# The recurrence's state-reading matmuls widened from 64x32 to 64x64 tiles

## The chip, the cores and the metric

The kernel runs on one core of one Trainium2 chip, in one launch. The metric is device time in microseconds (us), the median of three runs. The profile is of one execution, whose time is given beside its span.

## What is computed

Two blocks of two layers each are run one after the other on 512 tokens of width 1024. The first block has feed-forwards, an mLSTM layer and a dilated attention layer. The second block's layers mix a bidirectional RWKV-7 recurrence (6 heads of 64), a grouped-query attention and a neighbourhood attention; a context of 256 tokens goes through the same recurrence first and hands its end states on. What the change touches is the recurrence, which the reference writes as a scan over tokens in both directions:

```python
S_f, y_f = lax.scan(_rwkv7_step, S0_f, (r, decay[:, :, 0], kd[:, :, 0], v, kk, bd[:, :, 0]))
S_b, y_b = lax.scan(_rwkv7_step, S0_b, (r, decay[:, :, 1], kd[:, :, 1], v, kk, bd[:, :, 1]),
                    reverse=True)
return S_f, S_b, y_f + y_b
```

Each step multiplies a 64x64 state per head by its decay, takes out what the state holds along one direction and adds new key-value products.

## The kernel before

The kernel does the recurrence in chunks of 32 tokens. `rwkv_a`, `rwkv_b` and `rwkv_c` prepare, for a direction r, all that doesn't depend on the state: among it `zk`, three tiles (one for two heads, one head in the upper and one in the lower 64 partitions) of 128 x n with 32 columns for each chunk, copied out of PSUM at L1907; `be`, the tokens' write vectors; and `UV`, the values, in rows of 64 of which 32 are the state's correction.

`rwkv_d` (from L1910) then runs the chain, step by step, for the forward direction r = 0 and the backward direction r = 1 side by side. In a step a direction takes chunk g (ascending for r = 0, descending for r = 1) and does this:

- a first group of six matmuls (three tiles, two halves, L1932): 64 partitions of `zk`, the chunk's 32 columns, as the stationary operand, and the state S as the moving one, 64 columns. The product lands in 32 rows of the PSUM tile `pw`, at row 0 or 64;
- on GpSimd, `keep`, the state times the chunk's decay (L1934);
- on VectorE, the subtraction of `pw` from `UV` in two halves (L1941);
- a second group of six matmuls on 64x64 tiles (L1946), `be` against the corrected `UV`, into `pn`;
- on VectorE, the sum of `pn` and `keep`, which is the new S (L1950).

After every fourth step, where outputs are wanted, the y matmuls follow: 24 a direction with the states kept from the four steps (64x32 tiles, L1967) and 12 with `UV` on 128x64 tiles (L1973). All of these are float32 matmuls, which TensorE runs in two passes, each with a weight load and a matmul of its own in the profile.

`rwkv_d` is run four times: for the context of either layer (8 steps; the first layer's with outputs) beside the first block's feed-forward, and for the latents of either layer (16 steps) beside the attention.

The order of instructions is not that of the program's text. All operations are recorded, and a planner (`simulate`, L485, called by `schedule`, L588) puts them in order for the five engines: a list scheduler with costs for each operation (`_cost`, L408), which goes backward and forward three times. For TensorE it adds 0.14 us where the tile shape changes (`RETILE`, L274), and among ready matmuls it prefers one of the current shape if its priority is within 3.0 us (`STAY`, L278) of the most urgent. It also hands out the working tiles, kind "t" (64 slots), "S" (16), "ps" (8) and others (`SLOTS`, L265), and may put a plain copy of 60 columns or more on ScalarE or on VectorE (L381). Since every instruction is issued from one place, all lines of the profile are L632.

Of the kernel before, what the change touches and what calls it, by code (L numbers as in the profile page):

```python
# [16 lines left out]
P = 128  # L17
# [618 lines left out]
class Prog:  # L636
# [47 lines left out]
    def row(self):  # L684
        return self.t2((4, T))
# [1193 lines left out]
    def rwkv_c(self, d, q, r):  # L1879

        n, nb = d["n"], d["nb"]
        UV = d["UV"][r]
        q["zk"] = []
        for j in range(3):
            pb = [self.ps((P, nb, 64)) for _ in range(2)]
            for b in range(nb):
                for par in range(2):
                    for a in range(2):
                        self.mm(pb[par][64 * a:64 * a + 64, b], q["EB"][2 * j + par][:, 2 * b + a], UV[:, b, a, 2 * j + par])
            bv = self.t2((P, 2, nb, 64))  # L1890
            for par in range(2):
                self.act(bv[:, par], pb[par])
            pu, pz = self.ps((P, nb, 2, 64)), self.ps((P, n))
            for par in range(2):
                h, o = 2 * j + par, 64 * par
                x = self.t2((P, nb, 4, 32))
                self.mul(x, q["Z"][:, :, nb * h:nb * h + nb].rearrange("p t b -> p b t").unsqueeze(2).to_broadcast([P, nb, 4, 32]),
                         self.k("bd4").unsqueeze(1).unsqueeze(3).to_broadcast([P, nb, 4, 32]))
                x = x.rearrange("p b c t -> p b (c t)")
                for b in range(nb):  # L1900
                    self.mm(pu[:, b, par], x[:, b], bv[:, par, b])
                    self.mm(pz[o:o + 64, P * b:P * b + P], q["kt"][j][:, b, o:o + 64], x[:, b])
                for c in range(4):
                    ro = 64 * (c % 2 ^ par)
                    self.act(UV[ro:ro + 32, :, c // 2, h], pu[32 * c:32 * c + 32, :, par], scale=-1.0)
            zk = self.t2((P, n))
            self.act(zk, pz)  # L1907
            q["zk"].append(zk)

    def rwkv_d(self, d, qs, S):  # L1910

        n, nb, need_y = d["n"], d["nb"], d["need_y"]
        if need_y:
            d["y"] = [None] * nb
        both = [(j, par) for j in range(3) for par in range(2)]
        row = lambda c, par: 64 * (c % 2 ^ par)
        S = list(S)
        old, pw, pn = [{}, {}], [None] * 2, [None] * 2  # L1920
        for step in range(4 * nb):
            gs = (step, 4 * nb - 1 - step)
            keep = []
            for r, g in enumerate(gs):
                c = g % 4
                if step % 4 == 0:
                    ps = self.ps((P, 2, 3, 64))
                    pw[r], pn[r] = ps[:, 0], ps[:, 1]
                old[r][c] = S[r]
                for j, par in both:  # L1930
                    o, ro = 64 * par, row(c, par)
                    self.mm(pw[r][ro:ro + 32, j], qs[r]["zk"][j][o:o + 64, 32 * g:32 * g + 32], S[r][o:o + 64, j])  # L1932
                keep.append(self.new("S", (P, 3, 64)))
                self.nc.gpsimd.tensor_tensor(out=keep[r], in0=S[r], in1=qs[r]["D"][:, g].unsqueeze(2).to_broadcast([P, 3, 64]),  # L1934
                                             op=ALU.mult)
            for r, g in enumerate(gs):
                b, c = g // 4, g % 4
                for par in range(2):
                    ro = row(c, par)
                    u = d["UV"][r][ro:ro + 32, b, c // 2, par::2]  # L1940
                    self.tt(u, u, pw[r][ro:ro + 32], ALU.subtract)  # L1941
            for r, g in enumerate(gs):
                b, c = g // 4, g % 4
                for j, par in both:
                    o, ro = 64 * par, row(c, par)
                    self.mm(pn[r][o:o + 64, j], qs[r]["be"][j][g // 8][ro:ro + 64, g // 2 % 4, o:o + 64],  # L1946
                            d["UV"][r][ro:ro + 64, b, c // 2, 2 * j + par])
            for r in range(2):
                S[r] = self.new("S", (P, 3, 64))
                self.tt(S[r], pn[r], keep[r], ALU.add)  # L1950
            if not need_y or step % 4 < 3:
                continue

            py = [[self.ps((P, 3, 64)) for _ in range(2)] for _ in range(2)]
            rho, EQ = [], []
            for r, g in enumerate(gs):
                b = g // 4
                rho.append(self.load(self.t2((P, 3, P)), qs[r]["rho"][:, :, P * b:P * b + P].rearrange("j p t -> p j t")))
                EQ.append([self.load(self.t2((P, 3, 2, 64)), qs[r]["EQ"][par][:, :, 2 * b:2 * b + 2].rearrange("j p g x -> p j g x"))
                           for par in range(2)])  # L1960
            for r, g in enumerate(gs):
                b = g // 4
                for a in range(2):
                    for j in range(3):
                        for i, par in ((0, 0), (0, 1), (1, 0), (1, 1)):
                            o, cc = 64 * par, 2 * a + (i ^ par)
                            self.mm(py[r][par][32 * cc:32 * cc + 32, j], rho[r][o:o + 64, j, 32 * cc:32 * cc + 32],  # L1967
                                    old[r][cc][o:o + 64, j], start=(j == 0), stop=False, skip_group_check=True)
            for r, g in enumerate(gs):
                b = g // 4  # L1970
                for a in range(2):
                    for j, par in both:
                        self.mm(py[r][par][64 * a:64 * a + 64, j], EQ[r][par][:, j, a],  # L1973
                                d["UV"][r][:, b, a, 2 * j + par], start=False, skip_group_check=True)
            for r, g in enumerate(gs):
                b = g // 4
                first = d["y"][b] is None
                if first:
                    d["y"][b] = self.new("t", (P, 6, 64))
                for par in range(2):  # L1980
                    y = d["y"][b][:, par::2]
                    if first:
                        self.act(y, py[r][par])
                    else:
                        self.tt(y, y, py[r][par], ALU.add)
        return S
# [201 lines left out]
```

## Time and profile before

| | |
|---|---|
| median of three runs | 3187.92 us (3186.91 to 3193.73) |
| profiled execution | 3195.84 us |
| its span, first to last instruction | 3194.1 us |
| TensorE matmul busy | 3100.0 us, 97% |
| VectorE busy | 2334.6 us, 73% |
| ScalarE busy | 1567.7 us, 49% |
| GpSimd busy | 267.4 us, 8% |
| mean granted TensorE clock | 0.984 |

PE is TensorE's matmuls and PEld its weight loads, DVE is VectorE, ACT ScalarE, POOL GpSimd. A row of a timeline joins instructions of one kind that follow each other; its first number is where it starts, its second how long it lasts to the end of its last instruction, so that the start of the next row, and not the end of this one, tells when TensorE went on. A matmul's row names what it writes and reads (ps is PSUM, S the state, uv the tile UV, t a working tile) and its tile as partitions*columns of the stationary operand. The four recurrences lie at 1030 to 1120, 2150 to 2320, 2550 to 2720 and 3000 to 3140 us.

### The profile page before, as it was taken

To read this page: it belongs to the slowest core of one execution; us is meant where nothing else is said; L and a number is where in the kernel's file an instruction comes from. 1 tells how busy PE (TensorE), PEld (TensorE's weight loads), DVE (VectorE), ACT (ScalarE), POOL (GpSimd) and SP (SyncE) were. 2 spreads that over 40 slices of the span, in tenths; PEclk is the share of its full clock that TensorE was granted. 3 is DMA by queue.
4 is the path that set the end of the run, shared out by engine and by line. 5 is a ranking of instruction groups with operands and counts; after the bars stand their busy time and mean duration, and the time that the engine had idled before them with its cause. 6 is when DMAs were issued, how large, how long until landed. Compare 5 with 4: busy or idle time off the path is not lost. (4 is left out here: it accounts for less than half of the span.)

```text
span 3194.1 us, 55844 instructions
## 1 busy us (share of the span) xinstructions
PE 3100.0 (97%) x21142; PEld 2581.2 (81%) x21142; DVE 2334.6 (73%) x4908; ACT 1567.7 (49%) x3488; POOL 267.4 (8%) x245
## 2 busy tenths in 40 slices
PE   8999999999999999999999999999999899998997
PEld 6888888878887789888887788887777779876787
DVE  9945677485698676596666755877777888777977
ACT  5333464363445245333345734453455854655763
POOL 1000000000000101000001000000210022011011
PEclk9999999999999999999998999999999999999998
DMA  6633433133433343364332234222545244534342
GB/s 232 203 111 122 141 109 95 59 94 121 142 113 111 111 131 122 96 189 149 110 121 66 92 119 125 85 86 86 183 131 166 79 137 136 183 124 155 95 132 80
DMA packets 205382, 394.47 MB, mean 124 GB/s; under 512 B 20788, under 2 KB 105396, under 8 KB 204984
## 3 DMA queue, kind: packets, MB, share of 16 engines
q1 hardware_dynamic: 205112, 390.90, 39.1%
q8 instruction: 166, 2.72, 0.4%
q14 instruction: 104, 0.85, 0.1%
HBM read 340.21 MB, written 48.24 MB: 122 GB/s over the span
## 5 line engine op out<-in xcount | busy, mean ns | idle before, releaser
L632 PE MATMUL ps<-t,t 128*128 128x512 f32 (+7 forms) x15204 | 2805.5, 351 | 40.4 <-ACT t L632 17.2
L632 PEld LDWEIGHTS ps<-t,t 128*128 128x128 f32 (+3 forms) x15204 | 2296.4, 184 | 459.9 <-issue 37.6
L632 ACT ACTIVATE t<-raw 128x512 fp32r<-128x512 f32 (+1 forms) x932 | 547.9, 612 | 759.8 <-PE ps L632 466.2
L632 DVE TENSOR_TENSOR t<-raw,t 128x512 fp32r<-128x512 f32 (+2 forms) x962 | 628.8, 670 | 244.5 <-PE ps L632 160.1
L632 ACT ACTIVATE t<-t 128x512 f32<-128x512 f32 (+10 forms) x738 | 372.2, 522 | 428.2 <-DVE t L632 238.9
L632 DVE TENSOR_TENSOR t<-t,t 128x256 f32<-128x256 f32 (+7 forms) x818 | 415.4, 537 | 76.1 <-ACT t L632 47.1
L632 ACT ACTIVATE t<-ps 128x512 f32<-128x512 f32 (+7 forms) x437 | 208.8, 513 | 179.7 <-PE ps L632 174.5
L632 DVE TENSOR_TENSOR t<-ps,t 128x512 f32<-128x512 f32 (+3 forms) x274 | 178.4, 656 | 153.7 <-PE ps L632 147.1
L632 POOL TENSOR_TENSOR s<-s,const 128x4 f32<-128x4 f32 (+6 forms) x65 | 106.6, 1641 | 1726.6 <-DVE s L632 1719.4
L632 PE MATMUL ps<-const,t 128*128 128x128 f32 (+1 forms) x1116 | 185.9, 286 | 27.3 <-ACT t L632 11.1
L632 PEld LDWEIGHTS ps<-const,t 128*128 128x128 f32 x1116 | 135.2, 147 | 64.4 <-ACT t L632 25.6
L632 DVE SCALAR_TENSOR_TENSOR t<-ps,t 128x512 f32<-128x512 f32 (+3 forms) x229 | 147.1, 646 | 44.0 <-PE ps L632 43.2
L632 DVE SCALAR_TENSOR_TENSOR t<-raw,const,t 128x512 f32<-128x512 f32 x168 | 116.8, 744 | 0.7 <-DMA raw<-in_wmod_dram 0.4
L632 PE MATMUL ps<-uv,t 64*64 64x64 f32 (+1 forms) x2208 | 111.4, 228 | 4.4 <-ACT t L632 1.5
L632 PEld LDWEIGHTS ps<-uv,t 64*64 64x64 f32 (+1 forms) x2208 | 89.9, 136 | 31.1 <-issue 12.4
L632 ACT ACTIVATE t<-t,const 128x512 fp32r<-128x512 f32 (+3 forms) x155 | 96.3, 649 | 38.1 <-DVE t L632 27.6
L632 DVE SCALAR_TENSOR_TENSOR t<-t,t 128x512 f32<-128x512 f32 (+2 forms) x116 | 75.4, 653 | 38.1 <-ACT t L632 37.6
L632 POOL TENSOR_TENSOR S<-S,s 128x192 f32<-128x192 f32 x96 | 62.0, 651 | 426.1 <-DVE S L632 356.2
L632 ACT ACTIVATE uv<-ps 32x128 f32<-32x128 f32 (+1 forms) x239 | 76.1, 320 | 38.4 <-PE ps L632 24.5
L632 ACT ACTIVATE t<-ps,s,s 128x256 f32<-128x256 f32 (+1 forms) x140 | 88.9, 660 | 8.9 <-DVE s L632 8.5
L632 ACT ACTIVATE t<-ps,const 128x256 f32<-128x256 f32 (+1 forms) x100 | 56.6, 576 | 71.9 <-PE ps L632 71.5
L632 POOL TENSOR_TENSOR t<-t,s 64x512 f32<-64x512 f32 x36 | 49.2, 1375 | 477.3 <-ACT t L632 159.0
(89 smaller groups left out, 1466.4 us busy)
## 6 DMA issues: line engine op xcount, KB each, us to landing
raw<-in_wgu_dram SPq DMA_DIRECT2D x176, 512.0 KB, 4.0
raw<-in_win_dram SPq DMA_DIRECT2D x88, 512.0 KB, 4.0
raw<-in_wd_dram SPq DMA_DIRECT2D x128, 256.0 KB, 2.7
dram<-t SPq DMA_DIRECT2D x110, 256.0 KB, 2.2
raw<-in_wmod_dram SPq DMA_DIRECT2D x48, 512.0 KB, 4.1
t<-dram SPq DMA_DIRECT2D x179, 128.0 KB, 2.4
t<-dram SPq DMA_DIRECT2D x78, 256.0 KB, 3.0
dram<-t SPq DMA_DIRECT2D x114, 128.0 KB, 1.8
```

The lines of the kernel that those rows point to most:

```text
L632: getattr(getattr(tc.nc, op.eng), op.method)(*map(real, op.a), **{q: real(v) for q, v in op.k.items()})
```

## The change

The first group's stationary operand becomes 64 columns wide: the chunk's own 32 columns and the next chunk's 32 beside them. The product then fills 64 rows of `pw` instead of 32; only the first 32 are read, as before. The last chunk has no next one, so `rwkv_c` makes a small tile `zl` which holds the last chunk's 32 columns twice for each of the three tiles, by one copy each (128 x 64 elements). Both groups of a step are now on 64x64 tiles. The y matmuls, the constants of the planner and everything else stay.

```diff
@@ rwkv_c
-        q["zk"] = []
+        q["zk"], q["zl"] = [], self.new("t", (P, 3, 2, 32))
...
             self.act(zk, pz)
             q["zk"].append(zk)
 
+            self.act(q["zl"][:, j], zk[:, n - 32:].unsqueeze(1).to_broadcast([P, 2, 32]))
+
@@ rwkv_d
                 for j, par in both:
                     o, ro = 64 * par, row(c, par)
-                    self.mm(pw[r][ro:ro + 32, j], qs[r]["zk"][j][o:o + 64, 32 * g:32 * g + 32], S[r][o:o + 64, j])
+                    zk = qs[r]["zk"][j][o:o + 64, 32 * g:32 * g + 64]
+                    if g == 4 * nb - 1:
+                        zk = qs[r]["zl"][o:o + 64, j].rearrange("p a t -> p (a t)")
+                    self.mm(pw[r][ro:ro + 64, j], zk, S[r][o:o + 64, j])
```

## Rows read from the trace of the kernel before

**Rows 1.** The page: TensorE's busy time, and its granted clock in forty slices.
```profile
PE 3100.0 (97%) x21142; PEld 2581.2 (81%) x21142; DVE 2334.6 (73%) x4908; ACT 1567.7 (49%) x3488; POOL 267.4 (8%) x245
...
PEclk9999999999999999999998999999999999999998
```

**Rows 2.** Busy time by stage: stretch, length, engines' busy us, granted clock, DMA, GB/s.
```profile
1030.00:1120.00 90.00, 89.96 (x968) 71.49 (x968) 55.53 (x118) 29.75 (x68) 16.23 (x22) 1.00 0.40 119
2150.00:2320.00 170.00, 167.32 (x1150) 132.96 (x1149) 129.34 (x254) 66.91 (x134) 25.25 (x22) 1.00 0.42 134
2550.00:2720.00 170.00, 161.04 (x2268) 139.35 (x2268) 142.49 (x372) 89.04 (x230) 41.53 (x42) 0.99 0.44 135
3000.00:3140.00 140.00, 137.41 (x2173) 115.02 (x2172) 119.97 (x324) 85.11 (x224) 22.39 (x33) 1.00 0.44 132
3140.00:3195.00 55.00, 37.04 (x293) 35.77 (x291) 32.23 (x91) 18.58 (x42) 2.89 (x3) 0.84 0.15 49
```

**Rows 3.** TensorE's waits: for whom, us in total, times, longest us.
```profile
PE ps L632 <- ACT t L632: 31.3, 33, 3.5
PE ps L632 <- DVE t L632: 31.3, 16, 11.6
...
PE ps L632 <- DVE uv L632: 1.4, 3, 0.5
PE ps L632 <- DVE S L632: 1.4, 3, 0.7
```

**Rows 4.** TensorE's groups by shape: count, busy us, mean ns of one.
```profile
L632 PE MATMUL ps<-S,t 64*32 64x64 f32 x2112 | 66.2, 221 | 2.0 <-DVE S L632 1.4 <-ACT t L632 0.6
L632 PE MATMUL ps<-uv,t 64*64 64x64 f32 x1152 | 55.3, 227 | 1.2 <-DVE uv L632 0.9
...
L632 PEld LDWEIGHTS ps<-S,t 64*32 64x32 f32 x2112 | 48.5, 106 | 19.8 <-issue 9.1 <-DVE S L632 2.2 <-DVE t L632 1.6
L632 PEld LDWEIGHTS ps<-uv,t 64*64 64x64 f32 x1152 | 41.4, 133 | 17.3 <-issue 6.2 <-DVE uv L632 3.4 <-DVE t L632 2.3
```

**Rows 5.** TensorE's timeline in the first context's recurrence.
```profile
1041.60 0.49 PE L632 MATMUL ps<-t,t 128*128 128x512 f32 x1
1042.02 0.53 PE L632 MATMUL ps<-S,t 64*32 64x64 f32 x12
1042.48 1.20 PE L632 MATMUL ps<-t,t 128*128 128x512 f32 x4
1043.61 0.53 PE L632 MATMUL ps<-S,t 64*32 64x64 f32 x12
1044.06 0.56 PE L632 MATMUL ps<-uv,t 64*64 64x64 f32 x12
1044.56 1.42 PE L632 MATMUL ps<-t,t 128*128 128x512 f32 x5
```

**Rows 6.** The same timeline: a run with y, doubled runs of either shape.
```profile
1061.75 1.35 PE L632 MATMUL ps<-S,t 64*32 64x64 f32 x68
...
1065.79 0.74 PE L632 MATMUL ps<-uv,t 64*64 64x64 f32 x24
1066.47 0.50 PE L632 MATMUL ps<-t,t 128*128 128x512 f32 x1
...
2596.80 0.68 PE L632 MATMUL ps<-S,t 64*32 64x64 f32 x24
2597.40 0.39 PE L632 MATMUL ps<-t,t 128*128 128x256 f32 x1
```

**Rows 7.** The same timeline, first latent recurrence: the two shapes side by side.
```profile
2583.93 0.53 PE L632 MATMUL ps<-S,t 64*32 64x64 f32 x12
2584.39 0.33 PE L632 MATMUL ps<-uv,t 64*64 64x64 f32 x2
```

**Rows 8.** ScalarE's groups by shape: the copies nearest to 64 columns.
```profile
L632 ACT ACTIVATE t<-t 128x192 f32<-128x192 f32 x16 | 5.7, 358 | 4.2 <-DVE t L632 4.2
...
L632 ACT ACTIVATE t<-t 128x8 f32<-128x8 f32 x36 | 6.9, 214 | 23.9 <-DMA t<-dram 14.0 <-PE ps L632 6.5 <-issue 3.2
```

## The prediction

> **What bounds the kernel now.** I read the summary of the engines first, then a table of busy time by stage, then the groups of matmuls by shape, and last TensorE's own timeline inside the recurrence.
>
> The summary shows TensorE busy for 97% of the span and at its full clock in nearly every slice [rows 1]. The reader is to see that a change in TensorE's own occupancy is paid in full almost anywhere, and that a change on another engine is paid only where TensorE then waits. The recurrence runs in four stretches, two for the context (8 steps each) and two for the latents (16 steps each). In the context's two TensorE has no idle time worth naming (89.96 of 90 us and 167.32 of 170), because the feed-forward's matmuls fill its waits; in the latents' two it idles 9.0 of 170 and 2.6 of 140 us; in the tail behind the last one it idles 18 of 55 us and its mean clock falls to 0.84 [rows 2]. Of TensorE's waits, those that end on the recurrence's own VectorE results (the subtraction into uv and the sum into S) are 1.4 us each over the whole execution [rows 3]. So the chain's latency isn't the bound; the time that its matmuls take from TensorE is, with the switches from one tile shape to another counted in.
>
> **What a group costs today.** One direction's step issues six float32 matmuls to read the state (tiles 64x32) and six to write it (64x64), each as two passes: 12 instructions a group. There are 4 x (8, 8, 16, 16) steps' worth, that is 48 steps x 2 directions = 96 groups of either kind. The 1152 instructions of 64x64 with uv are the second groups; of the 2112 with S, 1152 are the first groups and 960 are the state part of the outputs y, which has the same 64x32 shape [rows 4] and keeps it.
>
> The timeline prices a group. A 64x32 group of 12 that starts at 1042.02 is followed by other work at 1042.48: 0.46 us. A 64x64 group of 12 at 1044.06 is followed at 1044.56: 0.50 us [rows 5]. Within that, the group is 0.53 or 0.56 us long to its end, its last instruction 0.22 (the mean of one in [rows 4]), so the last starts at 0.31 or 0.34, and the next run starts about 0.15 us after it. Inside a group a start follows the last by 0.03. A switch of tile shape thus costs about 0.12 us more than going on. The way in is dearer: 1041.60 to 1042.02 is 0.42 for one 128x512 matmul, while four of them and the switch behind them take 1.13 (1042.48 to 1043.61) [rows 5]; with 0.42 for the last, the other three take 0.24 each. The way in costs 0.18, the way out 0.12, an excursion from the big tiles 0.30 beside the group's own work.
>
> **The change, part by part.**
>
> First groups on 64x64 tiles: 96 groups x (0.50 - 0.46) = +3.8 us. The doubled runs say the same: 24 of 64x32 take 0.60 (2596.80 to 2597.40), 24 of 64x64 take 0.68 (1065.79 to 1066.47) [rows 6], 0.04 a group. The rows put 27 ns between the mean weight loads of 32 and of 64 columns (106 and 133), but 12 of them lengthen a group by 40 ns and not by 12 x 27 = 324 [rows 4, 5]: loads of different tiles lie beside each other.
> The Trainium skill, "TensorE: Matmul & The Clock Gate", section "LDWEIGHTS (loading the stationary operand)", says that a load's time goes by its columns, and so speaks against this edit, since half of the loaded columns are thrown away. The difference of the durations agrees; by that rule with no overlap the edit would cost the price of the first rival below, and the spacing in the timeline says an eighth of it.
>
> Switches that go: in the timeline of the four stretches a 64x32 run and a 64x64 run of the recurrence stand side by side in 40 places (3, 2, 17 and 18), as at 1043.61/1044.06 and 2583.93/2584.39 [rows 5, 7]. At 0.12 to 0.13 each: -5.0 us if the order stays. Had the joined groups also run beside each other like a 24-run (0.68 instead of 0.45 + 0.50), it would be 0.27 each, -10.8 us, with the 0.04 above already in it. I take -5.0: two groups of opposite directions need not lie on different quarters of the array.
>
> Switches that come: the outputs' y matmuls stay at 64x32, and today they share runs with first groups. Seventeen runs of 64x32 in the four stretches are longer than 24, as the 68 at 1061.75 [rows 6], so hold both kinds; about 37 shorter ones are neither 12 nor 24 long, and some hold both. Between 17 and 54 new borders x 0.12 = +2.0 to +6.5. I take 30: +3.7.
>
> The new order: the whole program is put in order again by the planner, which holds to a tile shape over up to 3 us of priority and now sees a first group and a second group of the other direction as the same shape. The runs of 64x32 and of 64x64 in the four stretches come to some 205, 162 excursions once the 40 neighbours are counted as one. Each further join saves an excursion, 0.30. From 0 (every group waits for VectorE's result between, as at 1042.02 to 1043.61) to 30 joins, -9.0. I take 8: -2.4.
>
> The copy of the last 32 columns (zl): 24 small copies on ScalarE or VectorE. The trace of before has none of 64 columns; the nearest are 128x192 at 358 ns and 128x8 at 214 [rows 8], so 5 to 9 us in total, on engines that TensorE's work covers. Only the backward direction's first step reads zl at once; there it adds one copy, 0.36 at most, in front of its first group, four times: 0 to +1.4 us, and whatever stands behind that group in TensorE's queue waits with it. I take 0, since the planner puts ready work before it. Without that cover it is the 1.4. The tile also holds one of 64 working slots through each recurrence, a second one until the first step; what comes late then is a prefetch. TensorE's waits for ScalarE's and VectorE's working tiles are 31.3 us each [rows 3]; a sixty-fourth of both is 1 us. I take 0, as the slots are short only in the two latent stretches; a gain from it I exclude.
>
> No DMA is added, and no dependence but on zl: the next chunk's columns come from the same copy as the chunk's own, and the extra 32 rows of PSUM lie in a region that nobody reads.
>
> Sum: +3.8 - 5.0 + 3.7 - 2.4 + 0 = +0.1 us. The profiled execution took 3195.84 with a span of 3194.1, 7.9 above the median 3187.92. So 3195.9 on its scale, 3188 on the median's.
>
> **The rivals.**
>
> Every weight load in line (slower): if 64 columns cost each of the 1152 loads its 27 ns in full, +31 us, 3219. Against it stands the 0.50 of the 64x64 groups, measured with just such loads [rows 5]. Chance 0.03.
>
> The y matmuls fall out of the recurrence's runs (slower): today they fill TensorE while the first group's tile shape is on. A piece of y that no longer finds its shape there becomes an excursion of its own, at 0.30 rather than a border's 0.12. There are 20 groups of y (960 / 48); with each in two pieces apart from everything: +3.8 - 5.0 + 40 x 0.30 = +10.8 us, 3199. It decides, that is takes the sum over 6.4 us, from 25 such pieces. For it: the rivalry of a shape that stays 64x32 is new. Against it: y is urgent only for the output, and a planner that may delay it can issue the 96 instructions of both directions in one run. Chance 0.25.
>
> The directions interlock (faster): the planner puts B of one direction behind A of the other in most steps. With 40 more joins than today: +3.8 - 5.0 + 2.0 - 40 x 0.30 = -11.2 us, 3177. For it: in the latent stretches this happens already in 35 places without any reward; against it: the context's stretches have 44 runs for 64 groups and little left to join. Chance 0.29.
>
> The order elsewhere shifts (either sign): TensorE idles 94 us of the span (3194.1 less 3100.0), some 14 of them in the four stretches, so 80 elsewhere, and slices there are below full clock [rows 1, 2]. A tenth of that moved is 8 us. I spread this over the other cases and widen the range by it.
>
> **How the numbers follow.** The measurement of this kernel can't tell less than about 0.2%, 6.4 us, from no change. My own case, the sum between -6 and +6, has 0.43; its own range is 3182 to 3194. The y case with the loads in line gives slower 0.28, the interlocking gives faster 0.29. The forecast is 3188; the range, from the faster rival to the slower one with a small margin for the order elsewhere, is 3175 to 3201. Faster 0.29, same 0.43, slower 0.28.
>
> **What would show it.** In the profile after, the groups by shape should have 960 instructions of 64x32 and 1152 new ones of 64x64 with S, at a mean load of 133 ns. The timeline should show runs of 64x64 in which S and uv follow each other without the 0.12; a first group of 12 alone should go on after 0.50. The y matmuls should stand in runs of 48 or 96: if they come in pieces of 2 to 24 between big tiles, the slower rival is right; if the excursions in the latent stretches fall well under today's 126 (161 runs less 35 neighbours), the faster one. The forecast is wrong in kind if the stretches outside the recurrence, above all the tail, move by more than the four stretches do.

## The result, and the profile after

The changed kernel takes 3226.26 us (median of 4 runs, 3217.89 to 3228.34) against 3188.99 of the kernel before on the same chip: a ratio of 1.0107, 95% interval 1.0093 to 1.0120. It is 1% slower where no change was forecast, and outside the range.

The page after, engines' busy time and TensorE's granted clock in forty slices (compare [rows 1]):

```profile
PE 3119.6 (97%) x21142; PEld 2592.9 (80%) x21142; DVE 2337.7 (72%) x4911; ACT 1574.2 (49%) x3509; POOL 279.8 (9%) x245
...
PEclk9999999999999999999998999999998999998998
```

TensorE issues as many instructions as before and is busy for the same share of a longer span. Its groups by shape after (count, busy us, mean ns; compare [rows 4]):

```profile
L632 PE MATMUL ps<-uv,t 64*64 64x64 f32 x1152 | 56.1, 228 | 3.5 <-DVE uv L632 3.5
L632 PE MATMUL ps<-S,t 64*64 64x64 f32 x1152 | 50.5, 227 | 2.1 <-DVE S L632 1.2 <-ACT t L632 0.9
L632 PE MATMUL ps<-S,t 64*32 64x64 f32 x960 | 25.6, 226 | 0.9 <-ACT t L632 0.8
...
L632 PEld LDWEIGHTS ps<-S,t 64*64 64x64 f32 x1152 | 38.7, 134 | 17.0 <-issue 6.9 <-DVE S L632 1.9 <-ACT t L632 1.5
```

The change does what it says: 1152 first-group instructions are now 64x64 with loads of 134 ns, 960 stay. Together the matmuls with S and uv on 64x32 and 64x64 tiles are busy for 132.2 us against 121.5 [rows 4]: 10.7 of the 32.5 us by which the profiled span grew (3194.1 to 3226.6) at most.

So the question is where in the span the rest lies. A landmark that every version has is the sum into S on VectorE; its first and last in each recurrence cut the span into stretches that mean the same in both kernels. Busy time by such stretches, before (the two context recurrences, the latents' first, the stretch between, the latents' second, the tail; columns as in [rows 2]):

```profile
1036.50:1108.90 72.40, 72.36 (x809) 56.88 (x807) 40.36 (x86) 17.73 (x35) 8.13 (x16) 1.00 0.33 99
...
2211.80:2285.00 73.20, 73.20 (x619) 56.38 (x619) 57.50 (x115) 32.73 (x54) 12.41 (x16) 1.00 0.45 147
...
2554.50:2673.10 118.60, 114.55 (x1877) 94.53 (x1877) 101.27 (x265) 67.59 (x181) 37.97 (x39) 1.00 0.49 151
2673.10:3021.00 347.90, 325.00 (x2492) 274.55 (x2492) 273.69 (x612) 212.02 (x481) 40.05 (x26) 0.96 0.42 135
3021.00:3134.70 113.70, 111.92 (x1882) 93.18 (x1878) 95.12 (x259) 67.92 (x179) 21.02 (x32) 1.00 0.45 137
3134.70:3194.10 59.40, 42.34 (x337) 41.07 (x336) 36.76 (x101) 18.58 (x42) 4.26 (x4) 0.86 0.15 50
```

And after:

```profile
1033.70:1107.50 73.80, 73.80 (x822) 57.80 (x820) 41.16 (x88) 16.68 (x32) 11.15 (x16) 1.00 0.34 103
...
2208.90:2279.70 70.80, 70.80 (x609) 54.98 (x608) 55.34 (x114) 31.55 (x52) 10.50 (x16) 1.00 0.44 143
...
2548.80:2674.70 125.90, 120.55 (x1892) 99.23 (x1891) 105.90 (x267) 68.40 (x184) 34.20 (x39) 0.97 0.49 151
2674.70:3034.80 360.10, 326.77 (x2485) 276.75 (x2483) 273.34 (x612) 216.64 (x491) 39.83 (x26) 0.94 0.39 127
3034.80:3168.10 133.30, 130.82 (x1903) 105.98 (x1902) 94.59 (x248) 69.66 (x187) 20.99 (x32) 0.95 0.40 122
3168.10:3226.60 58.50, 41.42 (x330) 40.15 (x328) 36.78 (x102) 18.88 (x43) 4.26 (x4) 0.85 0.15 50
```

Up to 2548.80 the changed kernel is ahead by 5.7 us, though two of the four recurrences are done by then. It loses 7.3 us in the latents' first recurrence, 12.2 in the stretch after it, in which the next recurrence has no more than its opening groups (12 instructions of either kind), and 19.6 in the second one, though the edit touches as many matmuls there as in the first, where the loss was 7.3. A price per matmul would show in all four recurrences, and nowhere else.

The stretch without a recurrence tells more. TensorE's work there is the same (2492 and 2485 matmuls) but it idles 33.3 us instead of 22.9. TensorE's waits in it, before, and then after:

```profile
PE ps L632 <- ACT t L632: 12.3, 12, 3.5
PE ps L632 <- DVE t L632: 5.1, 4, 2.2
```

```profile
PE ps L632 <- DVE t L632: 15.9, 9, 6.1
PE ps L632 <- ACT t L632: 14.7, 13, 3.5
```

The waits on VectorE's working tiles went from 5.1 to 15.9 us in a place that the edit hardly touches. What is different there is the order of the instructions, and `zl` in one of the 64 working slots.

### The profile page after: what moved, and what is told of

Same layout as the page of the kernel before. It is cut to its first block, busy times and chain, and to the rows that moved or that the text cites. A ratio compares the mean times of both kernels' runs of the same rounds, so it can differ in the third digit from the quotient of the medians.

```text
span 3226.6 us, 55919 instructions
## 1 busy us (share of the span) xinstructions
PE 3119.6 (97%) x21142; PEld 2592.9 (80%) x21142; DVE 2337.7 (72%) x4911; ACT 1574.2 (49%) x3509; POOL 279.8 (9%) x245
## 4 chain that ended last, share of the span: by engine, by line
PE 85%; DVE 7%; ACT 4%; issue 1%; POOL 1%; DMA 1%; POOLq 0%; ACTq 0%; SPq 0%; DVEq 0%
PE ps L632 85%; DVE t L632 5%; ACT t L632 3%; DVE big L632 1%; DVE tmp L632 1%; POOL s L632 1%; DVE s L632 1%; ACT big L632 1%; ACT uv L632 0%; DMA raw<-in_win_dram 0%; DMA dram<-t 0%; DMA t<-dram 0%; DVE uv L632 0%; POOL uv L632 0%; DMA t<-in_x_dram 0%
## 5 line engine op out<-in xcount | busy, mean ns | idle before, releaser
L632 PE MATMUL ps<-t,t 128*128 128x512 f32 (+6 forms) x15204 | 2813.8, 352 | 41.7 <-DVE t L632 20.6
L632 DVE TENSOR_TENSOR t<-raw,t 128x512 fp32r<-128x512 f32 (+1 forms) x962 | 627.8, 669 | 239.1 <-PE ps L632 159.0
L632 ACT ACTIVATE t<-ps 128x512 f32<-128x512 f32 (+8 forms) x441 | 211.3, 513 | 203.6 <-PE ps L632 190.7
L632 POOL TENSOR_TENSOR s<-s,const 128x4 f32<-128x4 f32 (+6 forms) x65 | 119.6, 1843 | 1764.2 <-DVE s L632 1676.0
L632 ACT ACTIVATE t<-t,const 128x256 f32<-128x256 f32 (+3 forms) x158 | 97.8, 647 | 37.5 <-DVE t L632 28.4
L632 ACT ACTIVATE t<-ps,s,s 128x256 f32<-128x256 f32 (+1 forms) x140 | 88.9, 661 | 13.7 <-DVE s L632 11.8
```

The lines of the kernel that those rows point to most:

```text
L632: getattr(getattr(tc.nc, op.eng), op.method)(*map(real, op.a), **{q: real(v) for q, v in op.k.items()})
```

## The experiments

Two theories to start with. A: the loss is the planner's new order of the whole program. B: the wide tiles cost in themselves, as in the first rival of the prediction, whose 3219 lies close to the result. The first two experiments cross the order of one kernel with the tiles of the other.

**The old order with wide tiles.** The plan is made with the first groups as they were; the wide operands are put in when the instructions are written out.

```diff
                     self.mm(pw[r][ro:ro + 32, j], qs[r]["zk"][j][o:o + 64, 32 * g:32 * g + 32], S[r][o:o + 64, j])
+                    if g < 4 * nb - 1:
+                        self.nc.ops[-1].swap = (pw[r][ro:ro + 64, j], qs[r]["zk"][j][o:o + 64, 32 * g:32 * g + 64])
...
-            real = lambda x: x.get() if isinstance(x, Ref) else x
+            op.a, op.k = ((op.swap[0],), dict(op.k, lhsT=op.swap[1])) if hasattr(op, "swap") else (op.a, op.k); real = lambda x: x.get() if isinstance(x, Ref) else x
```

> The order of all instructions is that of the kernel before, on every engine; only the first groups are 64 columns wide (the last chunk's, 8 of 96, stay at 32, so no copy is needed). Theory A (the loss is the planner's new order): the tiles themselves cost 88 x 0.04 = +3.5 us, less 37 or so switches x 0.12 = -4.5, plus 17 to 54 new borders to the y matmuls x 0.12 = +2 to +6.5: 3189 +1 to +6, that is 3190 to 3195 us. Theory B (the wide tiles cost in themselves, each weight load in line): 88 x 12 x 27 ns = +28 us, about 3217.

Measured: 3197.98 us against 3190.27 (12 and 17 runs), 1.0019 [1.0010, 1.0028]: +6.1 us by the ratio, between +3 and +9. That is theory A's end of the scale, though its 3190 to 3195 was 3 us too low for the median; theory B's 3217 is out. Busy time by the same four recurrences in this kernel:

```profile
1035.10:1108.60 73.50, 73.50 (x817) 57.92 (x813) 40.52 (x85) 17.61 (x35) 7.37 (x16) 1.00 0.31 96
2210.70:2284.20 73.50, 73.50 (x619) 56.93 (x618) 57.66 (x115) 32.73 (x54) 12.46 (x16) 1.00 0.44 147
2553.10:2672.80 119.70, 116.32 (x1876) 96.68 (x1876) 101.04 (x265) 67.87 (x181) 37.93 (x39) 1.00 0.49 151
2672.80:3020.60 347.80, 325.08 (x2495) 274.35 (x2495) 273.46 (x612) 212.09 (x481) 38.92 (x26) 0.96 0.42 135
3020.60:3138.00 117.40, 115.06 (x1881) 95.94 (x1878) 95.78 (x258) 67.74 (x179) 20.46 (x32) 1.00 0.43 132
```

With the order held, the four recurrences grow by 1.1, 0.3, 1.1 and 3.7 us, 6.2 in all, and the stretch between the last two by -0.1: the growth is where the edit is. (The rest of this execution's span is 2.9 us shorter; executions of the kernel before lie up to 7.7 us apart.) The terms can be read off, since the instructions are the same, run by run. Two pairs of groups in the kernel before, which take 0.95 us each to the next work (1043.61 to 1044.56 in [rows 5], and this one):

```profile
1045.91 0.56 PE L632 MATMUL ps<-uv,t 64*64 64x64 f32 x12
1046.41 0.53 PE L632 MATMUL ps<-S,t 64*32 64x64 f32 x12
1046.86 1.66 PE L632 MATMUL ps<-t,t 128*128 128x512 f32 x6
```

The same two in the old order with wide tiles (the rows between, in which S and uv alternate, left out):

```profile
1042.19 0.39 PE L632 MATMUL ps<-S,t 64*64 64x64 f32 x6
1042.37 0.27 PE L632 MATMUL ps<-uv,t 64*64 64x64 f32 x2
...
1042.87 1.43 PE L632 MATMUL ps<-t,t 128*128 128x512 f32 x5
1044.22 0.56 PE L632 MATMUL ps<-uv,t 64*64 64x64 f32 x12
1044.62 0.52 PE L632 MATMUL ps<-S,t 64*64 64x64 f32 x12
1045.07 1.21 PE L632 MATMUL ps<-t,t 128*128 128x512 f32 x4
```

The first pair, a first group and then a second one, now takes 0.68, as a run of 24 does: the two issue in alternation. The other, a second group and then a first one, takes 0.85. So a switch that goes is worth 0.10 in one order of the pair and 0.27 in the other, with the wide group's 0.04 counted in. The Trainium skill, "TensorEngine Tiling (Array Packing)", section "Tiling Modes", says that changing the tiling mode drains TensorE and changing only the tile doesn't. The trace agrees as to time: without the change the same pairs take 0.10 to 0.27 us less; a drain itself isn't in its records. On the other side is a run that held y matmuls, before and then in the old order with wide tiles:

```profile
1066.90 1.68 PE L632 MATMUL ps<-S,t 64*32 64x64 f32 x76
1068.51 2.80 PE L632 MATMUL ps<-uv,t 128*64 128x64 f32 x66
```

```profile
1065.64 2.21 PE L632 MATMUL ps<-S,t 64*32 64x64 f32 x76
1067.79 2.80 PE L632 MATMUL ps<-uv,t 128*64 128x64 f32 x66
```

The last row of S joins both shapes under one name. Its 76 instructions now take 2.15 us; the same 76 took 1.61 before, since first groups and y alternate in the old order and each of four borders is now a switch, at about 0.12 once 0.08 for the two wide groups is taken off. In a run of 24, of which 12 became wide, one border cost more: 0.95 us (1031.40 to 1032.35) against 0.61 (1032.91 to 1033.52), so about 0.30 likewise. Counted over the trace there are 44 such borders, and 783 changes of shape in all against 760: at the prediction's prices +23 x 0.12 = 2.8, and 88 x 0.04 = 3.5, together 6.3. That this meets 6.1 is in part luck: without the wide groups' 0.04, single switches are worth 0.12 to 0.31 on both sides of the balance.

**The new order with narrow tiles.** The plan of the changed kernel, copies included; only the operands are 32 columns wide again, put in by the same line as above.

```diff
                     self.mm(pw[r][ro:ro + 64, j], zk, S[r][o:o + 64, j])
+                    zn = qs[r]["zl"][o:o + 64, j, 0] if g == 4 * nb - 1 else qs[r]["zk"][j][o:o + 64, 32 * g:32 * g + 32]
+                    self.nc.ops[-1].swap = (pw[r][ro:ro + 32, j], zn)
```

> The order of all instructions is that of the changed kernel, with its copies; only the first groups are narrow again (64x32, 32 columns). Theory A: the loss stays, 3218 to 3232 us, even a little more than the changed kernel where the planner set first and second groups side by side and a switch now stands between. Theory B: the loss goes, 3189 to 3200.

Measured: 3227.62 us, 1.0113 [1.0100, 1.0126]. The loss stays in full with not one wide tile in the kernel. The last two stretches in it:

```profile
2673.50:3033.30 359.80, 326.78 (x2482) 276.38 (x2480) 273.36 (x612) 216.35 (x491) 39.84 (x26) 0.94 0.40 127
3033.30:3169.10 135.80, 132.48 (x1903) 106.78 (x1902) 94.78 (x248) 69.81 (x187) 20.41 (x32) 0.91 0.39 119
```

359.8 and 135.8 us, like the changed kernel's 360.1 and 133.3. Theory B has fallen: the wide tiles are worth +6 us in the old order and about nothing (3226.3 less 3227.6) in the new.

**Which part of the edit moves the order.** One kernel has the wide tiles without the copies, the other the copies without the wide tiles; both are planned anew. Only the added lines of `rwkv_d` are shown.

```diff
+                    m = 64 if g < 4 * nb - 1 else 32
+                    self.mm(pw[r][ro:ro + m, j], qs[r]["zk"][j][o:o + 64, 32 * g:32 * g + m], S[r][o:o + 64, j])
```

> Wide first groups planned as 64x64, but the last chunk's stay at 64x32, so that the 24 copies and their two working tiles are gone. If the copies and their slots are what spoils the order: back to 3185 to 3197 us. If the planner's new view of the tile shapes is: 3215 to 3235. If neither and any disturbance of the planner moves the time: somewhere between 3175 and 3240, unlike both.

```diff
+                    zk = qs[r]["zk"][j][o:o + 64, 32 * g:32 * g + 32]
+                    if g == 4 * nb - 1:
+                        zk = qs[r]["zl"][o:o + 64, j, 0]
+                    self.mm(pw[r][ro:ro + 32, j], zk, S[r][o:o + 64, j])
```

> First groups narrow as before and planned as 64x32; only the 24 copies are added, and the last chunk reads its 32 columns from them. If the copies and their slots spoil the order: 3215 to 3235 us. If the tile shapes do: 3187 to 3195. If any disturbance of the planner moves the time: somewhere between 3175 and 3240.

Measured: 3214.48 us, 1.0075 [1.0057, 1.0093], without the copies; 3204.76, 1.0042 [1.0029, 1.0055], with the copies alone. Neither half alone is the culprit: both are slower than before, by 24 and 13 us, and neither repeats the 19.6 us in the last recurrence (their last sums into S come at 3144.4 and 3145.6, the changed kernel's at 3168.1). The copies alone fit the third of the outcomes written down beforehand and no other. The run without copies doesn't decide by itself: its 3214.5 lies 0.5 below the range for the planner's new view of the shapes, well within its interval. So there is a new question: is anything special about this edit, or does every disturbance of the planner cost as much?

**Disturbances that have nothing to do with the edit.** One constant of the planner is moved a little, in the kernel before and in the changed one. Theory A1: the order of the kernel before is a favourable one, and any other costs 10 to 40 us, wide tiles or not. Theory B1: the wide tiles, which the planner takes for one shape with the second groups, make it choose badly.

```diff
-AGAIN = 50.0
+AGAIN = 55.0
```

> The kernel before with nothing changed but one of the planner's constants that has no bearing on tile shapes (how far back the later rounds look, 50 to 55). Theory A1 (the order of the kernel before is a favourable draw, and any disturbance of the planner costs some 10 to 40 us, wide tiles or not): 3200 to 3230 us. Theory B1 (it is the wide tiles, seen by the planner as one shape with the second groups, that spoil the order): 3185 to 3197.

> The changed kernel with the same constant at 55. Theory A1: another draw, 3195 to 3235 us, above or below its twin with narrow tiles by chance, with some 6 us for the wide tiles. Theory B1: 3215 to 3235, and 25 to 40 above its twin.

```diff
-STAY = 3.0
+STAY = 3.5
```

> The kernel before with the planner holding to a tile shape over 3.5 us instead of 3.0. Theory A1: 3200 to 3230 us. Theory B1: 3185 to 3200.

> The changed kernel with the planner holding to a tile shape over 3.5 us. Theory A1: another draw, 3195 to 3235 us, above or below its twin by chance. Theory B1: 3215 to 3240, and 25 to 40 above its twin.

The same with a constant moved less, and with the price of a switch:

```diff
-STAY = 3.0
+STAY = 3.2
```

> The kernel before with the planner holding to a tile shape over 3.2 us instead of 3.0. Theory A1 (the order of the kernel before is a favourable draw): again above it, 3200 to 3225 us. Theory B1 (only wide tiles spoil the order): 3185 to 3200, which the two narrow draws so far, 3218 and 3211, speak against.

> The changed kernel with the same 3.2 us. Theory A1: 3195 to 3235 us, within 20 us of its narrow twin, either side. Theory B1: 25 to 40 us above its twin.

```diff
-RETILE = 0.14
+RETILE = 0.13
```

> The kernel before with the planner pricing a switch of tile shape at 0.13 us instead of 0.14 (0.12 is what the timeline shows). Theory A1: 3195 to 3225 us. Theory B1: 3185 to 3200.

> The changed kernel with a switch priced at 0.13 us. Theory A1: 3195 to 3235 us, within 20 us of its narrow twin, either side. Theory B1: 25 to 40 us above its twin.

Measured, medians in us, and the ratio to the kernel before with its interval:

| planner's constants | narrow tiles | wide tiles | wide less narrow |
|---|---|---|---|
| as they are | 3189.0 | 3226.3, 1.0107 [1.0093, 1.0120] | +37 |
| AGAIN 55 | 3218.4, 1.0084 [1.0069, 1.0099] | 3212.3, 1.0062 [1.0045, 1.0079] | -6 |
| STAY 3.5 | 3211.1, 1.0061 [1.0046, 1.0076] | 3209.2, 1.0054 [1.0039, 1.0069] | -2 |
| STAY 3.2 | 3211.4, 1.0065 [1.0049, 1.0082] | 3204.9, 1.0043 [1.0028, 1.0058] | -6 |
| RETILE 0.13 | 3210.2, 1.0062 [1.0047, 1.0077] | 3227.6, 1.0119 [1.0101, 1.0137] | +17 |

All four disturbed versions of the kernel before are slower than it, by 19 to 27 us, with no wide tile in them. Their wide twins lie below them in three cases of four. Theory B1, which asked for 25 to 40 above the twin, is out; A1 holds in all eight. Without the first row the four narrow orders average 3212.7 and the four wide ones 3213.5.

Where an order loses is not always the same. The ends of the four recurrences (last sum into S, us):

| | first | second | third | fourth | span |
|---|---|---|---|---|---|
| before | 1108.9 | 2285.0 | 2673.1 | 3134.7 | 3194.1 |
| after | 1107.5 | 2279.7 | 2674.7 | 3168.1 | 3226.6 |
| before, AGAIN 55 | 1114.8 | 2292.9 | 2728.3 | 3184.2 | 3215.6 |
| before, STAY 3.5 | 1116.7 | 2296.8 | 2726.3 | 3151.7 | 3213.6 |
| after, STAY 3.2 | 1106.6 | 2277.3 | 2663.1 | 3137.0 | 3199.2 |

Five of the eight disturbed versions end the latents' first recurrence at 2718.7 to 2728.3, the changed kernel at 2674.7.

How an order loses can be counted over the profiled traces. In each of the eleven new orders TensorE idles for longer (98.7 to 112.4 us against 94.0), all but one have more changes of shape (up to 817 against 760), and some are busy for longer at the lower clock. For the changed kernel an estimate from these counts is +12.9 us of idle time, +9.6 for the clock (half of the difference between 102.6 us busy at the lower level and 83.3 before), 47 more changes at 0.12 to 0.18 and 96 wide groups at 0.04: 32 to 35, against the span's 32.5. The narrow kernel with RETILE 0.13 has eleven changes of shape fewer than before and is still slower: 13.5 of idle time, 0.9 for the clock and -1 to -2 for the changes, 12 to 13 against 12.8. Over the thirteen versions that were profiled beside the kernel before, this sum, with 0.15 for a change, is within 4 us for eleven, and 5 to 8 too high for the wide ones at STAY 3.2 and AGAIN 55. These are accounts of one execution each, not causes that were tested one by one.

No version beats the kernel before; the best of the others in its median is the old order with wide tiles, 3198.0.

## Why the prediction was wrong

**The bound** held: TensorE is busy for 96 to 97% of the profiled span in each version.

**The wide groups, +3.8 us**, right. In the changed kernel a first group alone:

```profile
3096.53 0.56 PE L632 MATMUL ps<-S,t 64*64 64x64 f32 x12
3097.02 0.66 PE L632 MATMUL ps<-t,t 128*64 128x128 f32 x8
...
3107.87 0.74 PE L632 MATMUL ps<-S,t 64*64 64x64 f32 x24
3108.54 0.66 PE L632 MATMUL ps<-const,t 128*128 128x128 f32 x4
```

0.49 for 12 and 0.67 for 24, against the 0.50 and 0.68 that the 64x64 groups before promised. The rival with every load in line (and with it the reading of the load rule that adds 27 ns a load) is refuted by the old order with wide tiles, which has 1056 such loads for 6 us in all; that its 3219 lay near the result is luck.

**The switches that go and come** had a price, 0.12, that is right only in the middle, and wrong counts. The 0.27 a pair that was set aside, for groups of opposite directions that run beside each other, is what a first group followed by a second one shows; the other order shows 0.10 (0.14 without the 0.04 of the wide group). The old order with wide tiles has 66 changes between 64x32 and 64x64 where the kernel before has 43, 44 of them between a first group and y. So 21 of the neighbours that I took for first-group pairs are gone, not 40 (the others, mostly y beside a second group, stay), and 44 borders came, not 30. The sum without a new order was +3.8 - 5.0 + 3.7 = +2.5; it measures +6.1.

**The new order, -2.4 us, is the step that failed.** I took from the planner's rule that it would join more groups, between nothing and -9 us. The whole new order measures +28 (3226.3 less 3198.0, wide tiles in the new and in the old order; the new one has the copies and eight more wide groups with it). By the profiled spans, 29.3 apart, 19.7 of it lie in the four recurrences, where the term belongs. It isn't even the right sign: runs of the recurrence's matmuls between other work are 177 in the changed kernel against 163 before. The planner orders 26,800 operations at once, by priorities taken from the finish times of its last pass over all of them (`schedule`), and joins of the recurrence are no aim of its own. That this is why they got fewer is argued from the code, not shown.

**The order elsewhere** was named, sized at a tenth of TensorE's idle time (8 us), and spread over both signs. Outside the four recurrences the changed kernel is 9.6 us longer than the old order with wide tiles, so the size was near. But the sign wasn't open for an order as a whole: all eleven other orders that were run lost, 19 to 27 us in the four versions with nothing but a constant moved, which is what to expect where a kernel's order is the best among many. Whether its constants were chosen for that isn't shown; that they give the fastest of twelve orders is.

**The copies** at nothing: 254 ns each on ScalarE (22 of them, 5.4 us in all) and 172 on VectorE (2), and the first two recurrences in the new order are not late. Their slot's price can't be told from the order's.

**The other rivals and the signs.** The y matmuls stand in 45 runs in the changed kernel, 14 of them with no first or second group beside them; the second rival was to decide from 25. Excursions in the latents' recurrences went up, from 120 to 132 between first and last sum, so the directions don't interlock as the third rival had it. Against the kernel before, the four recurrences grew by 25.9 us and all the rest by 6.6: the sign of a forecast wrong in kind, more change outside than inside, didn't come.

What makes an order slower in the changed kernel can be read, but was not tested one by one. Against the old order with wide tiles the latents' first recurrence is 6.2 us longer, the stretch between 12.3, the last one 15.9. In the stretch between, idle time accounts for 10.6 of it. In the last there is none to speak of (2.5 us); there 34 more changes of shape than in the old order (206 against 172) are worth an estimated 4 to 6 us, at 0.12 for a way out and 0.18 for a way in, and a spell at the lower clock up to 6.9, half of 13.7. Why the loss is largest in the second layer's recurrence stays open.

## What to carry over

Where a scheduler orders the whole program, hold the order fixed to price an edit, and price the new order by itself, by moving something that has no meaning: here the edit was worth +6 us and the reordering +28 (by the other way round, +37 for the reordering with narrow tiles and about nothing for the tiles). Where the kernel's order is already the best of many, as here, a new one is to be put down not at zero but at a loss, of 13 to 38 us in these runs; one or two such meaningless moves tell beforehand whether it is. A result that matches a rival's number is no evidence for it before the rival's mechanism has been taken away once.

## What the runs showed of the hardware

TensorE's granted clock stayed at half for 13.7 us in which its records show it busy without a gap. Busy time in two stretches of the changed kernel, at the start of its last recurrence (stretch, length, PE, PEld, DVE, ACT, POOL, granted clock, DMA, GB/s):

```profile
3020.00:3042.00 22.00, 19.03 (x223) 14.48 (x222) 21.47 (x57) 16.23 (x42) 0.51 (x1) 1.00 0.35 110
3042.00:3055.70 13.70, 13.70 (x74) 11.91 (x74) 4.71 (x11) 4.88 (x13) 0.51 (x1) 0.50 0.15 45
```

Before it fell to 1.2 GHz the engine had idled 3.0 of 22 us in short pieces; for the 13.7 us at that level it is busy throughout, with matmuls of 64 and 128 columns. The same recurrence in the kernel before stays at 2.4 GHz (1.00). Over the whole span the mean granted clock is 0.979 in the profiled execution of the changed kernel and 0.984 before, and in the mean over its executions each of the eleven new orders is below the kernel before (0.979 to 0.984 against 0.985). A new order can thus cost more than its gaps.
